# Seven quarter products for the gates and ups of a SwiGLU, and its second product in four parts

## The chip, the core and the metric

The kernel runs on one core of a Trainium2 chip. The metric is the device time of one execution, in microseconds (us). Before the change it is 2462.51 us, the median of 3 runs (2462.24 to 2464.69). The profile comes from one further execution, of 2461.3 us.

The core has a matrix engine, TensorE (PE in the profile, with its weight loads as PEld), and four others: VectorE (DVE), ScalarE (ACT), GpSimd (POOL) and SyncE (SP), whose queue issues the transfers from memory here. Each engine runs its own instructions in order and waits on semaphores for the others. A matmul multiplies a stationary 128x128 block (the weight load) with a moving block of 128 rows and up to 512 columns, and adds into a bank of PSUM of 128x512 floats.

## The reference

Two layers of a streaming encoder, 512 tokens, 1024 channels, in single precision. What bears on the change is the feed-forward block, which stands at the start and at the end of each layer, four times in all:

```
x = x + 0.5 * swiglu(rms_norm(x, norm_ffn1[l]), ffn1_wi[l], ffn1_wo[l])
...
def swiglu(x, w_in, w_out):
    gate, up = jnp.split(x @ w_in, 2, axis=-1)
    return (jax.nn.silu(gate) * up) @ w_out
```

Here w_in is 1024 x 5632 (2816 gates and 2816 ups) and w_out is 2816 x 1024. Between the two feed-forward blocks of a layer stand a mixer (a recurrent part, attention in chunks and a pooling) and a cross attention; the change leaves them as they are.

## The kernel before

Everything is kept channels by tokens: x is eight tiles of 128 channels x 512 tokens. Products in full precision are made of three matmuls: each operand is split into a high part (`hi`, a copy on ScalarE into the type F32R) and the rest (`lo`, a subtraction on VectorE), and `mm3` (L155) adds hi·hi, hi·lo and lo·hi into one bank. `split` (L140) makes such a pair, and every split of a 128x512 tile is one instruction on ACT and one on DVE. All instructions of the helpers show under the helper's line: L69 (`tt`, two tensors on DVE), L72 (`stt`, a tensor times a scalar, then a tensor), L75 (`act`), L78 (`mm`).

`ffn` (L261) works as follows. `norm` (L249) splits x times the gains into eight pairs (`hhi`, `hlo`); the tokens' factor 1/rms is left out here, is worked out while the first products run (`rstd`, L236), and is multiplied in afterwards, as the tile `r`. Then come 22 values of f, one for each 128 hidden channels. For each, `proj` makes the gates (`pg`) and then the ups (`pu`): `weights` (L144) loads 128 x 1024 weights in one transfer of 512 KB into one of two `raw` tiles, splits them in two halves of 512 columns into `whi` and `wlo` (three buffers each), and eight times three matmuls with 512 moving columns follow. So one f is 48 matmuls of 128x512. DVE multiplies both banks with `r`, ACT takes the silu, DVE multiplies gate and up, and the result is split into `fhi` and `flo`, kept for all 22 f. After the last f, the second product goes over the eight output tiles m: 22 times three matmuls into `po`, then `update` (L215), which adds half of the bank to x[m], stores it for ffn1, and starts the sum of squares for the next norm (a square on ACT, an addition on POOL).

The instructions are not issued in the order in which the code writes them. The framework's scheduler lists them when the program is built: on each engine what is ready comes first, and of several ready ones that which the code wrote first; a tile's buffer is given out again when its last reader is done. Each engine then keeps to that list. So the splits of the next weights are listed between the epilogue's instructions of the f before. The tiles `raw` (2 buffers), `whi` and `wlo` (3 each), the scratch tiles `t` (8) and the PSUM banks (8, by the tags in `ROT`, L92) set how far ahead the list can go.

Of the kernel before, what the change touches and what calls it, by code (L numbers as in the profile page):

```python
# [9 lines left out]
F32R = mybir.dt.float32r  # L10
AF = mybir.ActivationFunctionType
# [3 lines left out]
P = 128  # L15
T = 512
D = 1024
DEPTH = 2
KD = 8
FF = 2816  # L20
KF = FF // P
# [9 lines left out]
REL_MAX = 256  # L31
LEAD, DENSE_RATE, ATT_RATE = 15, (1.0, 0.61, 0.98), 0.65
TURN_RATE = (0.5, 0.9)

PAR = {}
_n = 0
# [17 lines left out]
def trunk(tc, I, out, depth=DEPTH):  # L54
    nc = tc.nc
    ctx = ExitStack()
    with ctx:
        const = ctx.enter_context(tc.tile_pool(name="const", bufs=1))
        wp = ctx.enter_context(tc.tile_pool(name="wp", bufs=1))
# [6 lines left out]
        mult, add, sub = ALU.mult, ALU.add, ALU.subtract  # L66

        def tt(o, a, b, op, eng=None):
            (eng or nc.vector).tensor_tensor(out=o, in0=a, in1=b, op=op)  # L69

        def stt(o, a, s, b, op0, op1):
            nc.vector.scalar_tensor_tensor(out=o, in0=a, scalar=s, in1=b, op0=op0, op1=op1)  # L72

        def act(o, i, f, **k):
            nc.scalar.activation(out=o, in_=i, func=f, **k)  # L75

        def mm(o, w, x, start=True, stop=True):
            nc.tensor.matmul(o, lhsT=w, rhs=x, start=start, stop=stop)  # L78

        def t2(name, shape=None, dt=F32):  # L80
            return tp.tile(shape or [P, T], dt, tag="t", name=name, bufs=8)
# [4 lines left out]
        def xslot(name):  # L86
            return hp.tile([P, T], F32, tag="x", name=name, bufs=8)

        def bank(tag, name):
            return psp.tile([P, T], F32, tag=tag, name=name, bufs=1 if tag in ("po", "ch") else 2)  # L90

        ROT = ("acc", "iv", "sm", "po", "acc", "iv", "sm", "ch")  # L92

        def b2(name):
            return bp.tile([P, T], F32, tag="b", name=name, bufs=6)
# [14 lines left out]
        x = [xslot("x") for _ in range(KD)]  # L110
        ahead = []

        def load_raw(ap, n, step=1024):
            raw = wp.tile([P, 1024], F32, tag="raw", name="raw", bufs=2)
            for c in range(0, n, step):
                nc.sync.dma_start(out=raw[:, c:min(c + step, n)], in_=ap[:, c:min(c + step, n)])
            return raw
# [9 lines left out]
        def pc(l, n, j=0):  # L127
            o, w = PAR[n]
            return par[:, l, o + j:o + j + 1]
# [10 lines left out]
        def split(o_hi, o_lo, src):  # L140
            act(o_hi, src, AF.Copy)
            tt(o_lo, src, o_hi.bitcast(F32), sub)
# [12 lines left out]
        def mm3(p, w, v, first, last):  # L155
            (wh, wl), (vh, vl) = w, v
            mm(p, wh, vh, first, False)
            mm(p, wh, vl, False, False)
            mm(p, wl, vh, False, last)

        def proj_steps(p, ap, nk, acts, first=True, last=True):
            done = 0
            for k0 in range(0, nk, 8):
                n = min(8, nk - k0)
                w = weights(ap[:, k0:k0 + n].rearrange("p k m -> p (k m)"), n * P)
                for k in range(n):
                    s = slice(k % 4 * P, k % 4 * P + P)
                    hi, lo = w[k // 4]
                    mm3(p, (hi[:, s], lo[:, s]), acts[k0 + k], first and done == 0, last and done == nk - 1)
                    done += 1  # L170
                    if k % 2:
                        yield
# [19 lines left out]
        def proj(*a, **k):  # L192
            for _ in proj_steps(*a, **k):
                pass
# [8 lines left out]
        def square_in(k):  # L203
            if k == 0:
                a = tp.tile([P, T], F32, tag="ssa", name="ssa", bufs=1)
                act(a, x[k], AF.Square)
                ssq["a"] = a
            else:
                q = t2("sq")
                act(q, x[k], AF.Square)  # L210
                tt(ssq["a"], ssq["a"], q, add, nc.gpsimd)

        x_dram = dram.tile([KD, P, T], F32, name="xs")

        def update(k, p, scale=None, spill=False, fetch=None):  # L215

            if fetch is not None:
                x[k] = fetch
                nc.sync.dma_start(out=x[k], in_=x_dram[k])
            if scale is None:  # L220
                tt(x[k], x[k], p, add)
            else:
                stt(x[k], p, scale, x[k], mult, add)
            if spill:
                nc.sync.dma_start(out=x_dram[k], in_=x[k])
            square_in(k)
# [9 lines left out]
        def rstd(bcast=True, tag="sm"):  # L236

            rt = const.tile([P, 4], F32, tag="rtok", name="rtok", bufs=1)
            tok_rstd(ssq["a"], T, rt, 1.0, eps, tag)
            r = None  # L240
            if bcast:
                p = bank(tag, "psn")
                for i in range(4):
                    mm(p[:, i * P:(i + 1) * P], rt[:, i:i + 1].to_broadcast([P, P]), ident)
                r = tp.tile([P, T], F32, tag="rstd", name="rstd", bufs=1)
                act(r, p, AF.Copy)
            return r, rt

        def norm(l, gain):  # L249
            h = []  # L250
            for k in range(KD):
                g = pc(l, gain, k)
                hi = hslot("hhi")
                act(hi, x[k], AF.Copy, scale=g)
                lo = hslot("hlo")
                stt(lo, x[k], g, hi.bitcast(F32), mult, sub)
                h.append((hi, lo))
            return h


        def ffn(l, which):  # L261
            h = norm(l, f"norm_{which}")
            wi, wo = I[f"{which}_wi"][l], I[f"{which}_wo"][l]
            hid = []
            with tc.tile_pool(name="hid", bufs=1) as hidp:
                for f in range(KF):
                    pg = bank(ROT[2 * f % 8], "pg")
                    proj(pg, wi[2 * f], KD, h)
                    pu = bank(ROT[(2 * f + 1) % 8], "pu")
                    proj(pu, wi[2 * f + 1], KD, h)  # L270
                    if f == 0:
                        if which == "ffn1" and l == 0:
                            for k in range(KD):
                                square_in(k)
                        r, _ = rstd(tag="po")
                    z = t2("z")
                    tt(z, pg, r, mult)
                    act(z, z, AF.Silu)
                    u = t2("u")
                    tt(u, pu, r, mult)  # L280
                    tt(u, u, z, mult)
                    hi = hidp.tile([P, T], F32R, name=f"fhi{f}")
                    lo = hidp.tile([P, T], F32R, name=f"flo{f}")
                    split(hi, lo, u)
                    hid.append((hi, lo))
                for m in range(KD):
                    p = bank(ROT[(m + 4) % 8], "po")
                    proj(p, wo[m], KF, hid)
                    update(m, p, 0.5, spill=which == "ffn1")

        vf_dram = dram.tile([3, P, T], F32, name="vf")

# [505 lines left out]
        def cross(l):  # L798
            with tc.tile_pool(name=f"cx{l}", bufs=1) as cp:
# [151 lines left out]
                while live:  # L951
                    blocked = False
                    if "d" in live:
                        got = next(live["d"], live)
                        blocked = got is True
                        if got is live:
                            del live["d"]
                    credit += TURN_RATE[len(k) == 8]
                    while "a" in live and (credit >= 1 or blocked or "d" not in live):
# [17 lines left out]
        for l in range(depth):  # L977
            ffn(l, "ffn1")
            mixer(l)
            cross(l)  # L980
            ffn(l, "ffn2")
# [94 lines left out]
```

## Time and profile before

| What | Value |
|---|---|
| Median of the runs | 2462.51 us |
| The profiled execution | 2461.3 us, of which the span from the first instruction to the last is 2459.5 |
| PE busy | 2422.8 us, 14058 matmuls |
| DVE busy | 1296.4 us, 2361 instructions |
| ACT busy | 999.4 us, 1800 instructions |
| POOL busy | 190.1 us, 246 instructions |
| Read from memory, written | 215.89 MB, 7.08 MB |
| Granted TensorE clock | 0.998 of full speed |

The feed-forward blocks are easy to find in the trace, by the tiles `pg`, `pu` and `po`: 7 to 375 us, 868 to 1229, 1229 to 1590 and 2095 to 2456 us. A row of the trace's timeline gives an instruction's start, its duration, its engine and line, what it writes and reads, and in brackets how long the engine had been idle before it and what it had waited for. Matmuls overlap, so one takes 0.39 us from start to end while the next starts after 0.227 us; for a rate, starts are compared, or the chain of waits is read, whose rows give a start, a length and a count.

### The profile page before, as it was taken

The page shows a single profiled execution, that of the slowest core. Times are in us where ns is not written, and L with a number is a line of the kernel's source. Part 1 is how long each engine was busy: PE and PEld are TensorE (multiplying, and loading weights), DVE is VectorE, ACT ScalarE, POOL GpSimd, SP SyncE. Part 2 cuts the span into 40 slices and gives each one's busy share as a digit, 9 for nine tenths or more (in the row PEclk, how much of TensorE's full clock was granted, in tenths as well). Part 3 has the DMA queues.
Part 4 walks back from the last instruction along what each step waited for, and adds up shares of the span by engine and source line. Part 5 has one row for each costly group of instructions (what it writes and reads, how often), then busy time and mean ns, then how long its engine had stood idle before and what let it go on. Part 6 is the DMA issues. An engine that isn't in the chain of part 4 may idle for free.

```text
span 2459.5 us, 35629 instructions
## 1 busy us (share of the span) xinstructions
PE 2422.8 (99%) x14058; PEld 1997.1 (81%) x14058; DVE 1296.4 (53%) x2361; ACT 999.4 (41%) x1800; POOL 190.1 (8%) x246
## 2 busy tenths in 40 slices
PE   8999999999999999999999999999999999999999
PEld 6888887787689888888888888867876898888887
DVE  5444335767675644443444443367676755444432
ACT  4333334444465543333333333343444655433322
POOL 1000002101110100000000000021011101000000
PEclk9999999999999999999999999999999999999999
DMA  4233333210242223333333233322103422232333
GB/s 136 95 95 103 107 112 108 70 44 21 79 146 90 71 95 96 102 95 94 95 98 99 95 94 119 120 73 69 46 21 92 140 82 78 93 99 94 97 109 95
DMA packets 72503, 225.27 MB, mean 92 GB/s; under 512 B 8176, under 2 KB 13200, under 8 KB 72336
## 3 DMA queue, kind: packets, MB, share of 16 engines
q1 hardware_dynamic: 72336, 223.00, 28.8%
q8 instruction: 110, 1.80, 0.3%
q14 instruction: 57, 0.47, 0.1%
HBM read 215.89 MB, written 7.08 MB: 91 GB/s over the span
## 4 chain that ended last, share of the span: by engine, by line
PE 94%; DVE 3%; issue 1%; DMA 1%; ACT 1%; POOL 0%; POOLq 0%; ACTq 0%; DVEq 0%; SPq 0%
PE pu L78 20%; PE po L78 19%; PE pg L78 19%; PE pxq L78 5%; PE pin L78 4%; PE pout L78 3%; PE pxw L78 3%; PE pqk L78 3%; PE pxv L78 2%; PE pbvf L78 1%; PE pf L78 1%; PE ptt L78 1%; DVE wlo L69 1%; PE pr L78 1%; PE pxs L78 1%; PE pxo L78 1%
## 5 line engine op out<-in xcount | busy, mean ns | idle before, releaser
L75 ACT ACTIVATE whi<-raw 128x512 fp32r<-128x512 f32 (+1 forms) x806 | 492.5, 613 | 966.2 <-PE po L78 288.1
L69 DVE TENSOR_TENSOR wlo<-raw,whi 128x512 fp32r<-128x512 f32 (+1 forms) x806 | 551.4, 687 | 553.4 <-ACT whi L75 544.3
L78 PE MATMUL pg<-hhi,whi 128*128 128x512 f32 x704 | 275.6, 392 | 6.7 <-ACT whi L75 6.7
L78 PE MATMUL pg<-hlo,whi 128*128 128x512 f32 x704 | 275.6, 391 | 2.2 <-DVE hlo L72 2.2
L78 PE MATMUL pg<-hhi,wlo 128*128 128x512 f32 x704 | 274.7, 390 | 0.0
L78 PE MATMUL pu<-hhi,wlo 128*128 128x512 f32 x704 | 274.0, 389 | 0.7 <-DVE wlo L69 0.7
L78 PE MATMUL pu<-hlo,whi 128*128 128x512 f32 x704 | 273.9, 389 | 0.0
L78 PE MATMUL pu<-hhi,whi 128*128 128x512 f32 x704 | 273.9, 389 | 0.0
L78 PE MATMUL po<-fhi,whi 128*128 128x512 f32 x704 | 273.9, 389 | 0.0
L78 PE MATMUL po<-flo,whi 128*128 128x512 f32 x704 | 273.9, 389 | 0.0
L78 PE MATMUL po<-fhi,wlo 128*128 128x512 f32 x704 | 273.9, 389 | 0.0
L69 POOL TENSOR_TENSOR ssa<-ssa,sq 128x512 f32<-128x512 f32 x63 | 86.6, 1374 | 1221.3 <-ACT sq L75 1220.8
L78 PEld LDWEIGHTS pg<-hhi,whi 128*128 128x128 f32 x704 | 132.8, 189 | 34.2 <-ACT whi L75 6.7
L78 PEld LDWEIGHTS pg<-hlo,whi 128*128 128x128 f32 x704 | 132.6, 188 | 31.5 <-DVE hlo L72 4.7
L78 PEld LDWEIGHTS pu<-hhi,wlo 128*128 128x128 f32 x704 | 132.2, 188 | 28.6 <-DVE wlo L69 1.2
L78 PEld LDWEIGHTS pg<-hhi,wlo 128*128 128x128 f32 x704 | 132.6, 188 | 27.6 <-DVE wlo L69 0.3
L78 PEld LDWEIGHTS po<-fhi,wlo 128*128 128x128 f32 x704 | 132.2, 188 | 27.5
L78 PEld LDWEIGHTS po<-flo,whi 128*128 128x128 f32 x704 | 132.2, 188 | 27.5
L78 PEld LDWEIGHTS pu<-hlo,whi 128*128 128x128 f32 x704 | 132.2, 188 | 27.4
L78 PEld LDWEIGHTS pu<-hhi,whi 128*128 128x128 f32 x704 | 132.1, 188 | 27.4
L78 PEld LDWEIGHTS po<-fhi,whi 128*128 128x128 f32 x704 | 132.2, 188 | 27.3
L69 DVE TENSOR_TENSOR z<-pg,rstd 128x512 f32<-128x512 f32 x88 | 60.9, 692 | 133.9 <-PE pg L78 124.3
(305 smaller groups left out, 3971.9 us busy)
## 6 DMA issues: line engine op xcount, KB each, us to landing
raw<-in_ffn_wi_dram SPq DMA_DIRECT2D x175, 512.0 KB, 3.5
raw<-in_ffn_wo_dram SPq DMA_DIRECT2D x64, 512.0 KB, 3.5
raw<-in_w_in_dram SPq DMA_DIRECT2D x30, 512.0 KB, 3.5
raw<-in_ffn_wo_dram SPq DMA_DIRECT2D x32, 384.0 KB, 3.2
raw<-in_x_wk_dram SPq DMA_DIRECT2D x16, 512.0 KB, 3.5
raw<-in_x_wv_dram SPq DMA_DIRECT2D x16, 512.0 KB, 3.6
raw<-in_x_wq_dram SPq DMA_DIRECT2D x16, 512.0 KB, 3.6
raw<-in_w_qk_dram SPq DMA_DIRECT2D x12, 512.0 KB, 3.6
```

Source lines behind the costliest of these rows:

```text
L69: (eng or nc.vector).tensor_tensor(out=o, in0=a, in1=b, op=op)
L75: nc.scalar.activation(out=o, in_=i, func=f, **k)
L78: nc.tensor.matmul(o, lhsT=w, rhs=x, start=start, stop=stop)
```

## The change

For 20 of the 22 f (the first two stay as they were, `PLAIN`), gates and ups are made by a form of Strassen's algorithm. The weights of one f are a 2x2 matrix of blocks: gates and ups (rows) by channels 0 to 511 and 512 to 1023 (columns). The normed x is a 2x2 matrix too: the two halves of the channels by the two halves of the tokens. Eight quarter products become seven, at the cost of sums: `token_sums` forms four combinations of x (once for each block, eight split pairs `thi`, `tlo`), and `seven` forms four combinations of the weights for each f, splits seven blocks (`shi`, `slo`, seven buffers), runs seven products of 4 x 3 matmuls with 256 moving columns (`Q`), and combines the results on DVE while it reads the banks (`z`, `v`, `u`).

The second product is cut into four parts by f (`PARTS`: 0 to 4, 5 to 10, 11 to 16, 17 to 21). The part of some f runs beside the gates and ups of the next group: `seven` is a generator with seven stops, and from the fifth stop of a group (`WO_LEAD`) each stop lets `second` go one step, two f of one output tile. The last part stands alone at the end. Each part adds to x[m] by two DVE instructions, and the tokens' factor `r` comes in there (`seven` and `plain` leave it out of the ups). The hidden tiles are now a ring of 11 buffers instead of 22 tiles.

The diff, with lines cut that the text above says:

```diff
+PARTS, PLAIN, WO_RATE, WO_LEAD = (0, 5, 11, 17, 22), 2, 1.0, 4
...
+        Q = T // 2
+
         def ffn(l, which):
             h = norm(l, f"norm_{which}")
             wi, wo = I[f"{which}_wi"][l], I[f"{which}_wo"][l]
-            hid = []
             with tc.tile_pool(name="hid", bufs=1) as hidp:
-                for f in range(KF):
+                hid = []
+                r = None
+
+                def out(z, u):
+
+                    hi = hidp.tile([P, T], F32R, tag="fhi", name="fhi", bufs=11)
+                    lo = hidp.tile([P, T], F32R, tag="flo", name="flo", bufs=11)
+                    split(hi, lo, u)
+                    hid.append((hi, lo))
+
+                def plain(f):
+                    nonlocal r
                     pg = bank(ROT[2 * f % 8], "pg")
                     proj(pg, wi[2 * f], KD, h)
...
-                    tt(u, pu, r, mult)
+                    tt(u, pu, z, mult)
+                    out(z, u)
...
+                def token_sums():
+                    for k in range(4):
+                        ga, gb = pc(l, f"norm_{which}", k), pc(l, f"norm_{which}", k + 4)
+                        xa, xb = x[k], x[k + 4]
+                        b1 = t2("b1")
+                        act(b1, xa, AF.Copy, scale=ga)
+                        s1, s2 = t2("s12"), t2("s34")
+                        stt(s1[:, :Q], xa[:, Q:], ga, b1[:, :Q], mult, sub)
+                        stt(s1[:, Q:], xb[:, Q:], gb, s1[:, :Q], mult, sub)
+                        stt(s2[:, :Q], xb[:, Q:], gb, b1[:, Q:], mult, sub)
+                        stt(s2[:, Q:], xb[:, :Q], gb, s1[:, Q:], mult, sub)
+                        for s in (s1, s2):
+                            hi = hidp.tile([P, T], F32R, tag="thi", name="thi", bufs=8)
+                            lo = hidp.tile([P, T], F32R, tag="tlo", name="tlo", bufs=8)
+                            split(hi, lo, s)
+                            sums.append((hi, lo))
...
+                def seven(f):
+
+                    ra, rb = [load_raw(wi[2 * f + i].rearrange("p k m -> p (k m)"), 1024) for i in range(2)]
+                    a11, a12, a21, a22 = ra[:, :T], ra[:, T:], rb[:, :T], rb[:, T:]
+
+                    def parts(src):
+                        hi = hidp.tile([P, T], F32R, tag="shi", name="shi", bufs=7)
+                        lo = hidp.tile([P, T], F32R, tag="slo", name="slo", bufs=7)
+                        split(hi, lo, src)
+                        return hi, lo
+
+                    def sums_of(a, b, op):
+                        s = t2("ws")
+                        tt(s, a, b, op)
+                        return s
+
+                    def product(n, p, c, w):
+
+                        for k, v in enumerate(quarter(n)):
+                            s = slice(k * P, k * P + P)
+                            mm3(p[:, c * Q:c * Q + Q], (w[0][:, s], w[1][:, s]), v, not c and k == 0, (c or n == 1) and k == 3)
...
+                    w1 = parts(a11)
+                    w2 = parts(a12)
+                    s1 = sums_of(a21, a22, add)
+                    s2 = sums_of(s1, a11, sub)
+                    w6 = parts(s2)
+                    s4 = sums_of(a12, s2, sub)
+                    w3 = parts(s4)
+                    s3 = sums_of(a11, a21, sub)
+                    w7 = parts(s3)
+                    w5 = parts(s1)
+                    w4 = parts(a22)
+                    pa = bank("acc", "p1")
+                    product(1, pa, 0, w1)
+                    p1 = t2("p1")
+                    act(p1[:, :Q], pa[:, :Q], AF.Copy)
+                    yield
+                    pb = bank("iv", "p26")
+                    product(2, pb, 0, w2)
+                    yield
+                    product(6, pb, 1, w6)
+                    z = t2("z")
+                    tt(two(z), two(pb), twice(p1, 0), add)
+                    yield
+                    pb = bank("acc", "p37")
+                    product(3, pb, 0, w3)
+                    yield
+                    product(7, pb, 1, w7)
+                    v = t2("v")
+                    tt(two(v), two(pb), twice(z, 1), add)
+                    yield
+                    pb = bank("sm", "p54")
+                    product(5, pb, 0, w5)
+                    yield
+                    product(4, pb, 1, w4)
+                    tt(z[:, Q:], pb[:, :Q], v[:, :Q], add)
+                    tt(z, z, r, mult)
+                    act(z, z, AF.Silu)
+                    u = t2("u")
+
+                    tt(two(u)[:, ::-1], two(pb), twice(v, 1), add)
                     tt(u, u, z, mult)
...
+                    out(z, u)
+                    yield
+
+                def second(f0, f1, last, tags):
+
+                    for m in range(KD):
+                        p = bank(tags[m % len(tags)], "po")
+                        for g0 in range(f0, f1, 4):
+                            n = min(4, f1 - g0)
+                            raw = b2("wr")
+                            nc.sync.dma_start(out=raw[:, :n * P], in_=wo[m][:, g0:g0 + n].rearrange("p k m -> p (k m)"))
...
+                            split(hi[:, :n * P], lo[:, :n * P], raw[:, :n * P])
+                            for k in range(n):
+                                s = slice(k * P, k * P + P)
+                                mm3(p, (hi[:, s], lo[:, s]), hid[g0 + k], g0 + k == f0, g0 + k == f1 - 1)
+                                if k % 2:
+                                    yield
+                        t = t2("po")
+                        stt(t, p, 0.5, r, mult, mult)
+                        tt(x[m], x[m], t, add)
...
+                        yield
+
+                wos, credit = iter(()), 0
+                for f0, f1 in zip(PARTS, PARTS[1:]):
+                    for f in range(f0, f1):
+                        if f < PLAIN:
+                            plain(f)
+                            if f == 0:
+                                token_sums()
+                            continue
+                        for _ in seven(f):
+                            credit += WO_RATE
+                            while credit >= 1:
+                                credit -= 1
+                                next(wos, None)
+                    for _ in wos:
+                        pass
+                    wos, credit = second(f0, f1, f1 == KF, ("po", "ch") if f1 < KF else ROT[4:] + ROT[:4]), -WO_LEAD
+                for _ in wos:
+                    pass
```

More of the change, by code (lines that the diff above doesn't have):

```diff
@@ L279, in ffn @@
                     u = t2("u")
-                    tt(u, pu, r, mult)
-                    tt(u, u, z, mult)
[L282 to L289, printed above, removed]
+                    tt(u, pu, z, mult)
@@ new lines, in plain @@
+                    out(z, u)
+                sums = []
+                def token_sums():
[14 more added lines that the diff above has]
+                            sums.append((hi, lo))
@@ new lines, in quarter, with twice @@
+                def quarter(n):
+                    at = {1: (0, 0), 2: (4, 0), 3: (4, 1)}
+                    if n in at:
+                        k0, c = at[n]
+                        t = h[k0:k0 + 4]
+                    else:
+                        i, c = {5: (0, 0), 6: (0, 1), 7: (1, 0), 4: (1, 1)}[n]
+                        t = sums[i::2]
+                    return [(hi[:, c * Q:c * Q + Q], lo[:, c * Q:c * Q + Q]) for hi, lo in t]
+                def seven(f):
[14 more added lines that the diff above has]
+                            mm3(p[:, c * Q:c * Q + Q], (w[0][:, s], w[1][:, s]), v, not c and k == 0, (c or n == 1) and k == 3)
+                    def twice(t, c):
+                        return t[:, c * Q:c * Q + Q].unsqueeze(1).to_broadcast([P, 2, Q])
+                    two = lambda t: t.rearrange("p (c t) -> p c t", c=2)
+                    w1 = parts(a11)
[37 more added lines that the diff above has]
+                    tt(two(u)[:, ::-1], two(pb), twice(v, 1), add)
+                    tt(u, u, z, mult)
+                    out(z, u)
+                    yield
@@ new lines, in second @@
+                def second(f0, f1, last, tags):
[5 more added lines that the diff above has]
+                            nc.sync.dma_start(out=raw[:, :n * P], in_=wo[m][:, g0:g0 + n].rearrange("p k m -> p (k m)"))
+                            hi = wp.tile([P, 512], F32R, tag="whi", name="whi", bufs=3)
+                            lo = wp.tile([P, 512], F32R, tag="wlo", name="wlo", bufs=3)
+                            split(hi[:, :n * P], lo[:, :n * P], raw[:, :n * P])
[7 more added lines that the diff above has]
+                        tt(x[m], x[m], t, add)
+                        if last:
+                            if which == "ffn1":
+                                nc.sync.dma_start(out=x_dram[m], in_=x[m])
+                            square_in(m)
+                        yield
```

## The prediction, made before the changed kernel ran

> **What bounds the kernel now.** I read the page first: the busy shares, the slices and the shares of the chain that ended last.
>
> ```profile
> PE 2422.8 (99%) x14058; PEld 1997.1 (81%) x14058; DVE 1296.4 (53%) x2361; ACT 999.4 (41%) x1800; POOL 190.1 (8%) x246
> ...
> PE   8999999999999999999999999999999999999999
> PEld 6888887787689888888888888867876898888887
> DVE  5444335767675644443444443367676755444432
> ...
> PE 94%; DVE 3%; issue 1%; DMA 1%; ACT 1%; POOL 0%; POOLq 0%; ACTq 0%; DVEq 0%; SPq 0%
> ```
>
> PE is the chain. A busy PE need not stream at its rate, so the chain of waits in order of time comes next; its columns are start, length, what, count.
>
> ```profile
> 867.89 5.44 PE pg L78 x24
> 873.33 5.44 PE pu L78 x24
> 886.10 5.44 PE pu L78 x24
> ...
> 1109.14 119.68 PE po L78 x528
> ...
> 1942.42 5.51 PE pxq L78 x46
> ...
> 1973.91 14.87 PE pxq L78 x124
> ```
>
> A 512-column matmul takes 5.44 / 24 = 0.2267 us, and `po` has the same rate over 528 of them. A plain f (48 matmuls) is 10.88 us, a second product 119.68. A feed-forward block thus runs at PE's rate, with 1.9 us lost once, at `rstd` (886.10 less 878.77, less one 5.44). The last two rows price what the change adds: with 256 moving columns and a 128x128 weight load each, `pxq` runs at 14.87 / 124 = 0.1199 us.
>
> The table by stretches says how much of the other engines is free.
>
> ```profile
> core 0: us, PE busy (x) PEld busy (x) DVE busy (x) ACT busy (x) POOL busy (x), PEclk, DMA share, GB/s
> ...
> 1229.00:1470.00 241.00, 241.00 (x1073) 199.84 (x1072) 114.36 (x176) 86.70 (x138) 1.29 (x1) 1.00 0.31 97
> ```
>
> During gates and ups DVE is busy under half the time, and the clock is granted in full. Since the change loads DVE heavily, I looked at its timeline over one f (start, duration, instruction, idle before).
>
> ```profile
> 206.38 0.69 DVE L69 TENSOR_TENSOR z<-pg,rstd 128x512 f32<-128x512 f32 x1 [1.53 <-PE pg L78]
> 206.99 0.68 DVE L69 TENSOR_TENSOR wlo<-raw,whi 128x512 fp32r<-128x512 f32 x1
> 209.60 0.69 DVE L69 TENSOR_TENSOR wlo<-raw,whi 128x512 fp32r<-128x512 f32 x1 [1.93 <-ACT whi L75]
> 211.82 0.69 DVE L69 TENSOR_TENSOR u<-pu,rstd 128x512 f32<-128x512 f32 x1 [1.53 <-PE pu L78]
> 212.43 0.68 DVE L69 TENSOR_TENSOR wlo<-raw,whi 128x512 fp32r<-128x512 f32 x1
> 213.03 0.69 DVE L69 TENSOR_TENSOR u<-u,z 128x512 f32<-128x512 f32 x1
> 214.42 0.69 DVE L69 TENSOR_TENSOR flo<-u,fhi 128x512 fp32r<-128x512 f32 x1 [0.70 <-ACT fhi L75]
> 215.04 0.69 DVE L69 TENSOR_TENSOR wlo<-raw,whi 128x512 fp32r<-128x512 f32 x1
> ```
>
> Eight instructions per f. One lasts 0.69 us, but the next, where it doesn't depend on it, starts 0.605 us later (211.82, 212.43, 213.03). So 0.605 is the price in a dense row, 0.69 in a chain. The order also shows that the next weights' splits stand between the epilogue's instructions: the scheduler works ahead.
>
> **What PE saves.** A seven-product f has 7 x 12 = 84 matmuls of 256 columns: 84 x 0.1199 = 10.07 us against 10.88, a saving of 0.81. Over 20 f and four blocks: 80 x 0.81 = 64.6 us. The seventh product is worth less than an eighth because a half-wide matmul costs 53% of a whole one. The cheaper bound is exactly half, 0.1133 (1.36 us per f, 109 in all); the dearer would be serial weight loads, which the rate of `pxq` excludes. I take `pxq`: same types, same loads, same width.
>
> [...]
>
> The second product keeps its matmuls (4 parts, the same 528 of 512 columns), so it costs PE the same wherever it stands.
>
> **What DVE and ACT gain.** One seven-product f: 7 splits and 4 sums of weights, then `z`, `v`, half of `z`, `z` times `r`, `u`, `u` times `z`, `flo`: 17.5 instructions of 512 columns, 10.6 us at 0.605. Where no second product runs beside it, that is more than PE's 10.07. ACT has nine of these and a 256-column copy, by the rows below 9 x 0.63 + 0.42 = 6.1 us: hidden.
>
> ```profile
> 842.14 0.42 DVE L69 TENSOR_TENSOR wlo<-raw,whi 128x256 fp32r<-128x256 f32 x1
> ...
> 841.62 0.42 ACT L75 ACTIVATE whi<-raw 128x256 fp32r<-128x256 f32 x1 [1.26 <-DMA raw<-in_x_wo_dram]
> ...
> L75 ACT ACTIVATE fhi<-u 128x512 fp32r<-128x512 f32 x88 | 55.6, 632 | 124.6 <-DVE u L69 124.6
> ...
> L72 DVE SCALAR_TENSOR_TENSOR xk<-pxqt,par,xk 128x256 fp32r<-128x256 f32 x16 | 7.7, 482 | 3.5 <-ACT xk L75 3.5
> ```
>
> One step of the second product adds six matmuls, 1.36 us of PE; a whole m of six f is 4.08 us of PE over four steps and on DVE a split of 512, one of 256 (0.42 less the same overlap, 0.34), and two instructions of the update: 2.2 us. So a filled f (seven steps) is PE 10.07 + 7.1 = 17.2, DVE 10.6 + 3.8 = 14.4; with five-f parts 18.0 and 15.3. PE binds there. The steps: a part of five f has 8 x 3 = 24, one of six 8 x 4 = 32. Four stops of each group pass first, so unfilled are f = 2 to 4 (nothing to run yet), four stops of f = 5, f = 9 and 10, then six and four stops around f = 11 and 16, four at f = 17: some 7.6 f per block.
>
> **Where it stalls.** Both `raw` tiles now belong to one f. The second can be loaded again only when its last reader, the split of a22, is done.
>
> ```profile
> 20.93 3.46 DMA raw<-in_ffn_wi_dram
> ...
> SPq L116 <- DVE wlo L69: 1923.5, 386, 30.0
> ```
>
> The first row (chain of waits) is such a load on the path; the second says that SP's queue usually stands waiting for DVE to let go of a tile. So in an unfilled f there is a turn: load 3.5 us; then, before a22's split ends, nine weight instructions, `z`, `v` and two or three of the previous f's end, 13.5 x 0.605 = 8.2; and 0.7 for the chain s1, s2, ACT, `slo`, in which DVE finds less to do. That is 12.4 against PE's 10.07: PE loses 2.4 us per unfilled f once the slack is used. In a filled f the turn is some 3.5 us longer, 15.9, below PE's 17.2: slack grows again.
>
> At the start of a block comes the backlog of `token_sums`. By the 256-column row above (0.48 in a chain) one k is 4 x 0.48 + 2 x 0.605 = 3.1 us, four are 12.5. The rows there:
>
> ```profile
> 870.44 1.34 DVE L72 SCALAR_TENSOR_TENSOR hlo<-xs,par,hhi 128x512 fp32r<-128x512 f32 x1 [0.71 <-ACT hhi L75]
> ...
> 869.94 1.29 POOL L69 TENSOR_TENSOR ssa<-ssa,sq 128x512 f32<-128x512 f32 x1 [4.67 <-ACT sq L75]
> ```
>
> PE gives two plain f and `rstd`, 2 x 10.88 + 1.9 = 23.7 us; DVE has to do the last update and `hlo` (2), two times eight (9.7), the sums (12.5): 24.2. So DVE comes to f = 2 with nothing in hand beyond the first two splits. PE wants the split for product 6 after 2.88 us; three weight instructions, two of f = 1's end and ACT's copy make about 4.1: stall 1.2. The split of a22 is then done at 23.7 + 14 x 0.605 + 0.7 = 32.9, the load at 36.4, product 6's pair 4.2 later at 40.6 (3.0 for the chain, two instructions of f = 2's end ahead of it), where PE would be at 23.7 + 1.2 + 10.07 + 2.88 = 37.9: stall 2.7. Then 2.4 each at f = 4 and f = 5; from f = 6 on the fill restores slack. Sum 8.7 per block. At f = 9 to 11 and later I count none: three filled f save over 4 us, a tile's lead of one f, before two unfilled ones spend it.
>
> At the end of a block m follows m after 15 x 0.2267 = 3.4 us instead of 15, with 0.6 (split) + 0.2 + 1.2 (update) + 0.7 (`hlo`) of DVE, and POOL's 1.29 us addition beside it, during which `hlo` took 1.34. Close to balance: 1.5 us lost, bounds 0 and 4. The update's second instruction puts the last `hlo` at about 4 us behind the last matmul; the next stage's 21 matmuls of k = 0 to 6 (4.76 us) hide that. The hidden ring is no wait: f = 16 overwrites f = 5's buffer, whose readers end six stops earlier.
>
> Sum, against the profiled execution: 2461.3 - 64.6 + 4 x (8.7 + 1.5) = 2461.3 - 64.6 + 40.8 = 2437.5; the median stands 1.2 above it: **2438.7**.
>
> **The rivals.** (1) The scheduler hides the turn and the backlog, since lists put splits into every gap and PE can run other ready products; then only the end of a block costs: 2461.3 - 64.6 + 6 = 2402.7, so 2403.9 at the median. For it: before, PE never waits in these stages. Against: DVE has 10.6 us to do in 10.07.
>
> (2) Slower: the turn binds in the filled f too. SP's queue issues in order, and the second product's small loads (64 per block, where there were 24), each waiting for its own scratch tile, stand ahead of the `raw` load. If that puts 2 us on the turn, a filled turn is 15.9 + 2 = 17.9, with the ends' 0.7 of added chain 18.6 against 17.6 on average: 1.0 lost in each of some 13 f, and 2.4 in the unfilled 6 to 7: 29 per block, 2461.3 - 64.6 + 4 x 30.5 = 2519. It decides once filled turns pass 17.2; the change as a whole turns slower when a block loses over 16.2 us. For it: the long SP waits above. Against: 1.3 us of room.
>
> (3) Every DVE instruction costs its whole 0.69. Then an unfilled turn is 3.5 + 13.5 x 0.69 + 0.7 = 13.5 and a filled one 18.3: 3.4 x 6.5 + 0.7 x 13.5 = 32 per block, 2530. The starts at 0.605 speak against it. [...]
>
> (4) The matmuls don't get cheaper: 256 columns break even at 10.88 / 84 = 0.1295 us. If two readings of one bank or the mixing of widths costs that, 2461.3 + 41 = 2502. Every `pxq` row speaks against it.
>
> **How the numbers follow.** The forecast, with 4 to 14 us lost at the start and end of each block (2414 to 2454), 0.47; rival 1 0.27; rival 2 0.17; rival 3 0.04; rival 4 0.05. The range 2402 to 2500 takes in rival 1, the forecast and the milder half of rival 2. Measurement tells 0.2%, about 4.9 us, from no change. Faster: rival 1, 0.42 of the forecast, 0.02 of the others: 0.71. Within: 0.07. Slower: 0.22.
>
> **What would show it.** Right: matmuls of `p26`, `p37`, `p54` 0.120 us apart; PE idle a few us before product 6 of f = 3, 4 and 5 of each block, released by `slo` or DVE, with DVE dense and a `raw` load ending just before `ws`; no idle PE in filled f; DVE busy about 2000 us. Wrong: PE waiting in filled f (rival 2), starts on DVE 0.69 apart (3), matmuls at 0.13 (4), or no idle PE at all (1).

## The result and the profile after

The changed kernel takes 2476.06 us, the median of 4 runs (2474.78 to 2477.6), beside 2462.38 us for the kernel before, the median of 4 (2457.64 to 2464.69). The ratio is 1.0058, with an interval of 1.0041 to 1.0076: slower by 14 us, where the prediction had 24 faster. The helpers' lines are one higher than before (L70 `tt`, L73 `stt`, L76 `act`, L79 `mm`). First the page of the kernel after.

```profile
span 2475.8 us, 43241 instructions
...
PE 2397.7 (97%) x16938; PEld 2080.2 (84%) x16938; DVE 1929.0 (78%) x3537; ACT 1161.6 (47%) x2232; POOL 188.6 (8%) x246
...
PE   7999999999999989999989999999999999899999
...
PE 83%; DVE 10%; issue 2%; ACT 2%; DMA 2%; POOL 0%; POOLq 0%; ACTq 0%; DVEq 0%; SPq 0%
```

DVE has gone from 3% to 10% of the chain that ended last, and PE from 94% to 83%. The slices of PE dip at the start of the four blocks (7, 8, 8, 8). Laid out by blocks, from the first `pg` to the last `po`:

| Block | before | after |
|---|---|---|
| 1 | 368.1 | 369.3 |
| 2 | 360.9 | 362.7 |
| 3 | 360.9 | 364.9 |
| 4 | 360.9 | 361.6 |

The blocks are 7.5 us longer together instead of 64.8 shorter (80 x 0.81), so 72.3 us are lost inside them, and 8.8 more outside: 7.0 in the stretches from a block's last `po` to the next block's first `pg`, and 1.8 at the end of the kernel. Where the 72.3 lie, by the gaps between starts of successive matmuls beyond 0.1199 us (256 columns) and 0.2267 (512): f = 2 33.5 over the four blocks, f = 3 to 6 15.1, f = 12 5.4, the other seven-product f 9.7 (0.1 to 0.3 each), the last part of the second product 5.8, 2.6 at the start of block 3, which follows block 2 directly, and 0.2 in the plain f of block 1.

**The largest loss, f = 2.** The table by stretches of the kernel after, at the start of the second block (columns: length, busy time of PE, PEld, DVE, ACT and POOL with counts, granted clock, DMA share, GB/s):

```profile
880.00:892.00 12.00, 12.00 (x62) 10.17 (x61) 4.79 (x8) 6.81 (x10) 0.00 (x0) 1.00 0.24 82
892.00:898.00 6.00, 6.00 (x30) 5.03 (x29) 5.83 (x12) 4.90 (x10) 0.00 (x0) 1.00 0.44 129
898.00:904.00 6.00, 2.97 (x23) 2.54 (x22) 6.00 (x15) 3.92 (x7) 0.00 (x0) 1.00 0.00 0
904.00:910.00 6.00, 3.22 (x7) 2.14 (x8) 5.96 (x12) 2.72 (x6) 0.00 (x0) 0.57 0.17 50
```

Up to 892 us DVE is busy 40% of the time (4.79 of 12 us); from then on it is full, and only then PE runs dry. The work was there to be done earlier. What held it is in ACT's timeline of the same kernel:

```profile
891.44 0.63 ACT L76 ACTIVATE z<-z 128x512 f32<-128x512 f32 x1
...
892.60 0.71 ACT L76 ACTIVATE b<-xs,par 128x512 f32<-128x512 f32 x1
...
893.73 0.71 ACT L76 ACTIVATE b<-xs,par 128x512 f32<-128x512 f32 x1
```

`b<-xs,par` is the first step of `token_sums` for one k. It needs nothing but x, which was complete at 875.2, yet the first one starts at 892.60, 18.8 us into the block (which starts at 873.81), just behind the silu of f = 0. And the chain of waits:

```profile
891.44 0.64 ACT z L76
...
892.17 0.09 DVE u L70
...
893.41 0.89 DVE s L73 x2
...
905.18 0.68 DVE tlo L70
...
906.06 0.68 DVE u L70
...
906.78 3.45 PE po L79 x7
...
911.89 6.72 PE p L79 x56
```

So from 893 to 906 the path runs through DVE (`s`, `tlo`), and f = 1's `u` stands behind the sums. By the code's tags it frees the bank of PSUM that the next `po` use. PE's timeline has PE idle for 5.81 us before them, until that `u`:

```profile
906.78 0.80 PE L79 MATMUL po<-fhi,whi 128*128 128x512 f32 x1 [5.81 <-DVE u L70]
```

Then the clock: seven `po` of 512 columns take 3.45 us there, 0.49 each, where 56 `p` of 256 columns after 911.89 take 0.1200 each as predicted. The granted clock is 0.50 for 6.83 us from 904.86 on (0.57 over 904 to 910 above), and for as long in the same place of all four blocks; of the 8.4 us that f = 2 loses, some 2.4 are that (the starts in this stretch against 0.2267 and 0.1199).

**The end of a block.** First the timeline of POOL, whose addition closes each output tile, then that of DVE for two tiles, both of the kernel after:

```profile
1221.34 1.29 POOL L70 TENSOR_TENSOR ssa<-ssa,sq 128x512 f32<-128x512 f32 x1 [2.76 <-ACT sq L76]
1225.39 1.30 POOL L70 TENSOR_TENSOR ssa<-ssa,sq 128x512 f32<-128x512 f32 x1 [2.76 <-ACT sq L76]
1229.45 1.30 POOL L70 TENSOR_TENSOR ssa<-ssa,sq 128x512 f32<-128x512 f32 x1 [2.76 <-ACT sq L76]
```

```profile
1219.05 0.68 DVE L73 SCALAR_TENSOR_TENSOR po<-po,rstd 128x512 f32<-128x512 f32 x1
...
1221.43 1.36 DVE L70 TENSOR_TENSOR wlo<-wr,whi 128x128 fp32r<-128x128 f32 x1 [0.30 <-ACT whi L76]
1222.71 0.68 DVE L73 SCALAR_TENSOR_TENSOR po<-po,rstd 128x512 f32<-128x512 f32 x1
1223.31 0.68 DVE L70 TENSOR_TENSOR wlo<-wr,whi 128x512 fp32r<-128x512 f32 x1
1223.91 0.68 DVE L70 TENSOR_TENSOR xs<-xs,po 128x512 f32<-128x512 f32 x1
1224.51 0.74 DVE L73 SCALAR_TENSOR_TENSOR hlo<-xs,par,hhi 128x512 fp32r<-128x512 f32 x1
1225.90 1.34 DVE L73 SCALAR_TENSOR_TENSOR hlo<-xs,par,hhi 128x512 fp32r<-128x512 f32 x1 [0.65 <-ACT hhi L76]
1227.16 0.68 DVE L73 SCALAR_TENSOR_TENSOR po<-po,rstd 128x512 f32<-128x512 f32 x1
```

A tile comes every 4.06 us (1221.34, 1225.39, 1229.45) where PE needs 3.4. Two of the DVE instructions above start while POOL's addition runs, and both end shortly behind it: the split of 128 columns 0.16 us (1222.79, where POOL ends at 1222.63), `hlo` 0.55 us (1227.24, 1226.69). They take 1.36 and 1.34 us, where the same instructions take 0.28 (at 1219.65) and 0.74 (at 1224.51) without it. DVE falls behind tile by tile, and the next block pays at its start. The chain of waits there:

```profile
1242.71 1.34 DVE hlo L73
...
1244.09 0.73 PE pg L79 x2
```

The last `hlo` ends at 1244.05, 7.5 us behind the last matmul of the block (which starts at 1236.27; 0.23 more is an estimate of its end by the rate of 0.2267); the prediction had about 4, hidden by 4.76 us of other matmuls.

### The profile page after: what moved, and what is told of

Read it like the earlier page. It is cut to its first block, busy times and chain, and to the rows that moved or that the text cites. A ratio compares the mean times of both kernels' runs of the same rounds, so it can differ in the third digit from the quotient of the medians.

```text
span 2475.8 us, 43241 instructions
## 1 busy us (share of the span) xinstructions
PE 2397.7 (97%) x16938; PEld 2080.2 (84%) x16938; DVE 1929.0 (78%) x3537; ACT 1161.6 (47%) x2232; POOL 188.6 (8%) x246
## 4 chain that ended last, share of the span: by engine, by line
PE 83%; DVE 10%; issue 2%; ACT 2%; DMA 2%; POOL 0%; POOLq 0%; ACTq 0%; DVEq 0%; SPq 0%
PE p L79 29%; PE po L79 18%; PE pxq L79 6%; PE pin L79 4%; PE pxw L79 3%; PE pout L79 3%; PE pqk L79 3%; DVE wlo L70 2%; PE pbvf L79 1%; PE pu L79 1%; PE pf L79 1%; PE ptt L79 1%; DVE ws L70 1%; DVE s L73 1%; PE pg L79 1%
## 5 line engine op out<-in xcount | busy, mean ns | idle before, releaser
L79 PE MATMUL p<-thi,shi 128*128 128x256 f32 x1280 | 365.1, 286 | 5.1 <-ACT shi L76 5.0
L79 PE MATMUL p<-thi,slo 128*128 128x256 f32 x1280 | 360.0, 284 | 2.3 <-DVE slo L70 2.3
L79 PE MATMUL p<-tlo,shi 128*128 128x256 f32 x1280 | 361.4, 283 | 0.0
L70 DVE TENSOR_TENSOR wlo<-raw,whi 128x512 fp32r<-128x512 f32 (+3 forms) x294 | 209.7, 722 | 122.1 <-ACT whi L76 110.6
L79 PE MATMUL po<-fhi,whi 128*128 128x512 f32 x704 | 278.7, 400 | 25.1 <-DVE u L70 22.8
L79 PE MATMUL po<-fhi,wlo 128*128 128x512 f32 x704 | 278.3, 396 | 2.9 <-DVE wlo L70 2.5
L79 PE MATMUL po<-flo,whi 128*128 128x512 f32 x704 | 280.1, 398 | 0.0
L76 ACT ACTIVATE whi<-raw 128x512 fp32r<-128x512 f32 (+3 forms) x294 | 175.0, 602 | 215.8 <-PE pin L79 50.9
L79 PE MATMUL p<-hlo,shi 128*128 128x256 f32 x960 | 271.9, 283 | 0.0
L79 PE MATMUL p<-hhi,shi 128*128 128x256 f32 x960 | 271.9, 283 | 0.0
L79 PE MATMUL p<-hhi,slo 128*128 128x256 f32 x960 | 271.6, 283 | 0.0
L79 PEld LDWEIGHTS p<-thi,shi 128*128 128x128 f32 x1280 | 244.5, 191 | 30.7 <-ACT shi L76 23.5
L79 PEld LDWEIGHTS p<-thi,slo 128*128 128x128 f32 x1280 | 243.4, 191 | 10.3 <-DVE slo L70 6.6
L79 PEld LDWEIGHTS p<-tlo,shi 128*128 128x128 f32 x1280 | 244.9, 191 | 4.4
L76 ACT ACTIVATE shi<-ws 128x512 fp32r<-128x512 f32 x320 | 191.9, 627 | 120.3 <-DVE ws L70 118.5
L76 ACT ACTIVATE whi<-wr 128x512 fp32r<-128x512 f32 (+2 forms) x256 | 125.1, 492 | 247.0 <-PE po L79 160.2
L70 POOL TENSOR_TENSOR ssa<-ssa,sq 128x512 f32<-128x512 f32 x63 | 86.3, 1370 | 1775.9 <-ACT sq L76 1435.3
L70 DVE TENSOR_TENSOR slo<-ws,shi 128x512 fp32r<-128x512 f32 x320 | 210.6, 686 | 4.5 <-ACT shi L76 4.0
L70 DVE TENSOR_TENSOR wlo<-wr,whi 128x512 fp32r<-128x512 f32 (+2 forms) x256 | 143.7, 563 | 62.0 <-ACT whi L76 61.6
L76 ACT ACTIVATE shi<-raw 128x512 fp32r<-128x512 f32 x240 | 141.8, 622 | 101.2 <-DMA raw<-in_ffn_wi_dram 101.0
L79 PEld LDWEIGHTS p<-hhi,shi 128*128 128x128 f32 x960 | 183.6, 191 | 5.5 <-ACT shi L76 1.0
L79 PEld LDWEIGHTS p<-hlo,shi 128*128 128x128 f32 x960 | 183.8, 191 | 4.2
```

## The experiments

Theory A: the sums of f = 2 come late because the scratch ring `t` (8 buffers) is given out in the order in which the code asks, and `b1`, `s12` and `s34` ask behind `z` and `u` of f = 0, which wait for 1/rms. Theory B, the prediction's own: DVE simply has more to do at the start than PE gives it time for. A second question is what sets the period of an unfilled f (12.4 us), a third what the end costs.

**e1: own tiles for the sums.** They take buffers of `shi` and `slo`, which nothing uses yet.

```diff
-                        b1 = t2("b1")
+                        b1 = hidp.tile([P, T], F32, tag="slo", name="b1", bufs=7)
...
-                        s1, s2 = t2("s12"), t2("s34")
+                        s1, s2 = [hidp.tile([P, T], F32, tag="shi", name=n, bufs=7) for n in ("s12", "s34")]
```

> The changed kernel, only that token_sums takes its scratch tiles from the rings of shi and slo, which stand empty then, instead of from the ring t. Theory A: PE loses 8.4 us at f = 2 of each block because the ring t is handed out in the order in which the code asks: the first sum stands behind z and u of f = 0, and these wait for rstd, so DVE lies idle for some 15 us and has all sums to do at once. Then the first sum starts about 3 us after the block instead of 19, but ahead of the splits for f = 1, since the code writes it first: the loss goes from 8.4 to 3 to 6 us, 2455 to 2467 us in all. Theory B: the 12.5 us of sums are simply too much work for DVE before f = 2, whatever the order: 2473 to 2479 us.

Measured: 2464.12 us beside 2461.39, ratio 1.0014 (1.0004 to 1.0023). The loss of f = 2 fell from between 8.0 and 8.8 us per block to 0.3, so the ring was what held the sums. But now they are listed ahead of f = 1's weight splits, and the two plain f lose 18.4, 2.8, 4.7 and 4.5 us in the four blocks, where they lost 7.6, 0.2, 2.8 and 0.2. Freed from one place, the work stood in another place's way.

**e1b: the same, and the sums asked for after f = 1.**

```diff
-                            if f == 0:
+                            if f == 1:
                                 token_sums()
```

> As e1_own_tiles, and the sums are written behind f = 1 instead of f = 0, so that the splits for f = 1 go first and the sums fill DVE's gaps. Theory A: the loss at f = 2 falls from 8.4 to about 1.5 us per block, the stretches of half clock in the blocks go, 2476 - 28 = 2448 us. Theory B: 2473 to 2479 us, with the half clock still there.

Measured: 2447.11 us beside 2461.39, ratio 0.9947 (0.993 to 0.9964). ACT's timeline and the stretch of f = 2 in this kernel, whose second block begins at 868.97:

```profile
866.82 0.71 ACT L76 ACTIVATE b<-xs,par 128x512 f32<-128x512 f32 x1
...
873.72 0.71 ACT L76 ACTIVATE b<-xs,par 128x512 f32<-128x512 f32 x1
```

```profile
894.00:900.00 6.00, 6.00 (x42) 5.28 (x41) 5.89 (x10) 3.87 (x8) 0.00 (x0) 1.00 0.25 65
900.00:906.00 6.00, 6.00 (x52) 6.00 (x51) 3.95 (x7) 1.31 (x3) 0.00 (x0) 1.00 0.46 162
```

These are the first and the last of the four `b`: they start 2.2 us ahead of the block and 4.8 us into it, where in the change they start 18.8 and 25.5 us into it (899.32). PE has no gap, the clock stays at 1.00, and f = 2 loses 0.4 (2.8 in the first block). The plain f lose 1.0 us more per block (1.7 in the first, 0.6 in the third). DVE does the same work, so theory B falls: it was never too much, it was late. The gain over the change is 29 us.

**e3: one instruction for the last update.** The factor `r` goes into the hidden tiles of the last part again, and x[m] gets half of the bank in one instruction.

```diff
                     tt(u, u, z, mult)
+                    if f >= PARTS[-2]:
+                        tt(u, u, r, mult)
                     out(z, u)
...
-                        t = t2("po")
-                        stt(t, p, 0.5, r, mult, mult)
-                        tt(x[m], x[m], t, add)
+                        if last:
+                            stt(x[m], p, 0.5, x[m], mult, add)
+                        else:
+                            t = t2("po")
+                            stt(t, p, 0.5, r, mult, mult)
+                            tt(x[m], x[m], t, add)
```

> The changed kernel, only that the last part's hidden tiles are multiplied by r (one DVE instruction for each of five f), and so the last update is one DVE instruction per output tile instead of two. Theory: at the end of a block DVE sets the pace, 4.06 us per output tile against PE's 3.4; 0.6 less makes it 3.46, and the 4.4 us lost per block there and at the start of the next stage become about 1: 2476 - 14 = 2462 us. Rival: the pace is set by POOL's additions and by ACT's order, so output tiles still come every 4.0 us or more: 2473 to 2479 us.

Measured: 2462.82 us beside 2461.39, ratio 1.0007 (0.9997 to 1.0016), 13 us faster than the change. DVE's timeline of this kernel:

```profile
1213.27 0.68 DVE L73 SCALAR_TENSOR_TENSOR xs<-po,xs 128x512 f32<-128x512 f32 x1
...
1216.72 0.68 DVE L73 SCALAR_TENSOR_TENSOR xs<-po,xs 128x512 f32<-128x512 f32 x1
...
1220.17 0.68 DVE L73 SCALAR_TENSOR_TENSOR xs<-po,xs 128x512 f32<-128x512 f32 x1
```

A tile every 3.45 us, close to PE's own 3.40; the last part loses 0.1 us per block instead of 0.5 to 1.8, and the 2.6 at the start of block 3 are gone. One DVE instruction less per output tile, 32 in all (and 20 more beside the last gates and ups, where there is room), was worth 13 us. What a single profile cannot settle is how much of the rest lies outside the blocks: the stretches between blocks are 495 and 502 us here, 498 and 507 in the change, 493 and 505 in the kernel before.

**e5: the parts alone.** All 22 f stay plain, and no sums are made; the second product still comes in four parts.

```diff
-PARTS, PLAIN, WO_RATE, WO_LEAD = (0, 5, 11, 17, 22), 2, 1.0, 4
+PARTS, PLAIN, WO_RATE, WO_LEAD = (0, 5, 11, 17, 22), 22, 1.0, 4
...
-                            if f == 0:
-                                token_sums()
```

> The four-part second product alone: all 22 f are made the old way (eight quarter products, no sums of tokens), and each part runs behind its group. If the end of the block is what the parts cost, 4.4 us per block: 2462.4 + 18 = 2480 us. If the parts cost nothing by themselves and all losses come from the seven products: 2462 us.

Measured: 2478.53 us beside 2461.39, ratio 1.0073 (1.0058 to 1.0088). The parts alone cost 17 us, with DVE busy only 1402.1 us, so it isn't DVE's total that costs. Most of it lies at the blocks' ends, as e3 suggests: in e5's trace 5.5 us are lost in the last parts, 2.8 at the start of block 3 and 1.8 at the end of the kernel. The seven products on top of them bring 2.5 us of their 64.8.

**e7: e1b and e3 together.**

> The sums' own scratch tiles behind f = 1 (as e1b) and the single update in the last part (as e3) together. The two losses lie at opposite ends of a block, so the gains add: 2476 - 29 - 13 = 2434 us, faster than both kernels. If one gain only moves a wait that the other had hidden, 2440 us or more.

Measured: 2437.55 us beside 2461.28 (2431.94 to 2438.12), ratio 0.99 (0.9886 to 0.9915). This beats both kernels, by 24 us and by 38. The two remedies alone came to 29 and 13, so together they fall short of their sum by about 4, which is no more than the uncertainty (the interval of the ratio is 7 us wide). What is left in the blocks: 17.9 us in the first (7.3 of them were lost before the change), 9.3, 8.9 and 10.2 in the others, of which f = 3 to 6 make 3.1 and f = 12 1.4 to 2.5.

The next three start from e7 and ask about the period of an unfilled f. The row of one in e7 (f = 10 of the second block), in the table by stretches, whose counts take in matmuls that reach over its ends:

```profile
1004.75:1017.15 12.40, 12.40 (x95) 11.68 (x94) 11.01 (x18) 5.51 (x10) 0.00 (x0) 1.00 0.27 88
```

12.40 us as predicted, but PE isn't idle: besides the 84 matmuls of the f it runs about nine `po`, which the scheduler listed there.

**e8: the ups' weights in two transfers, into another ring.** If the `raw` tile sets the turn, this should shorten it.

```diff
-                    ra, rb = [load_raw(wi[2 * f + i].rearrange("p k m -> p (k m)"), 1024) for i in range(2)]
-                    a11, a12, a21, a22 = ra[:, :T], ra[:, T:], rb[:, :T], rb[:, T:]
+                    ra = load_raw(wi[2 * f].rearrange("p k m -> p (k m)"), 1024)
+                    wu = wi[2 * f + 1].rearrange("p k m -> p (k m)")
+                    a21, a22 = b2("a21"), b2("a22")
+                    nc.sync.dma_start(out=a21, in_=wu[:, :T])
+                    nc.sync.dma_start(out=a22, in_=wu[:, T:])
+                    a11, a12 = ra[:, :T], ra[:, T:]
```

> As e7_both, and the ups' weights of each f are loaded in two halves of 256 KB into two tiles of the ring b (six buffers) instead of into the second raw tile, so the load for the next f no longer waits for the last split of this one. Theory of the prediction (the raw tiles' turn of 12.4 us sets the unfilled f): f = 3 to 5 come every 11 us instead of 12.3, and 4 to 12 us are gained in all: 2422 to 2430. Rival: the turn is set by the ring t, because the first weight sum of an f asks for its tile behind the u of the f before: f = 3 to 5 still come every 12.3 us, 2431 to 2437.

Measured: 2453.21 us beside 2461.28, ratio 0.997 (0.9959 to 0.9982), 16 us worse than e7. f = 9 in this kernel:

```profile
996.80:1009.85 13.05, 10.59 (x86) 10.18 (x85) 12.24 (x22) 6.56 (x12) 0.00 (x0) 1.00 0.21 71
```

84 matmuls in 13.05 us, 2.5 of them idle: the turn got no shorter, and no `po` fills it any more. None of the 80 first weight sums waits for a load here. That the second product's weights now stand behind the ups' in one ring is the likely reason; it wasn't tried by itself.

**e9: the four sums of the weights in the other ring, `raw` as it was.**

```diff
-                        s = t2("ws")
+                        s = b2("ws")
```

> As e7_both, and the weight sums take their tiles from the ring b instead of t, so they need not wait for the u of the f before; the raw tiles stay two. If the ring t sets the turn of the unfilled f: f = 3 to 5 under 12 us, 2422 to 2430. If the raw load sets it: 12.3 us as before, 2431 to 2437; the second product's loads now stand behind the sums in ring b, which may cost some of PE's filling.

Measured: 2439.45 us beside 2461.28, ratio 0.9913 (0.9898 to 0.9927), the same as e7 within its uncertainty. f = 9 and 10 of the first block:

```profile
148.45:158.53 10.08, 10.08 (x86) 10.08 (x85) 9.24 (x16) 3.84 (x7) 0.00 (x0) 1.00 0.18 54
158.53:168.60 10.07, 10.07 (x86) 10.07 (x85) 9.33 (x16) 4.26 (x9) 0.00 (x0) 1.00 0.43 145
```

With the loads untouched, these two f take 10.08 and 10.07 us with PE full. DVE's timelines show the difference, at the start of f = 10 of the second block; first e7, then e9:

```profile
1005.09 0.68 DVE L70 TENSOR_TENSOR u<-p,v 128x512 f32<-128x512 f32 x1
...
1006.28 0.69 DVE L70 TENSOR_TENSOR ws<-raw 128x512 f32<-128x512 f32 x1
```

```profile
1004.08 0.69 DVE L70 TENSOR_TENSOR ws<-raw 128x512 f32<-128x512 f32 x1
...
1005.46 0.69 DVE L70 TENSOR_TENSOR v<-p,z 128x512 f32<-128x512 f32 x1
...
1008.81 0.68 DVE L70 TENSOR_TENSOR u<-p,v 128x512 f32<-128x512 f32 x1
```

In e7 the first sum of the next weights stands behind `u` of the f before, because both take their tile from ring `t` in the order of the code; in e9 it runs 4.7 us ahead of that `u`. So in the change and in e7 the ring sets the turn: of the 80 first sums (one for each seven-product f) none in the change and one in e7 waits for a `raw` load. In e9 22 of them do, among them those of f = 10 and f = 11 of the first block, in DVE's timeline:

```profile
155.18 0.69 DVE L70 TENSOR_TENSOR ws<-raw 128x512 f32<-128x512 f32 x1 [0.74 <-DMA raw<-in_ffn_wi_dram]
...
167.25 0.69 DVE L70 TENSOR_TENSOR ws<-raw 128x512 f32<-128x512 f32 x1 [0.71 <-DMA raw<-in_ffn_wi_dram]
```

They are 12.07 us apart (12.0 to 12.3 in the other blocks). The load's turn is thus real and nearly as long as the ring's, which hid it. PE runs at 10.07 here only by a lead that it spends: the first sum starts 11.9 us ahead of its f at f = 9, 3.2 at f = 10 and 1.3 at f = 11. Where there is no lead, at f = 4 of the second to fourth block, the first sum waits 0.6 to 0.9 us for its load. So the time is no better: the `po` that filled the 12.4 us now stand elsewhere, and f = 4 and 5 lose 1.9 to 4.1 each instead of 0.9 and 1.3. e8 takes only the turn of the ups' load away and e9 only the ring's; no run takes away both.

**e6: no pace.** The stops of `seven` no longer call `second`; each part is asked for only behind the whole group of f that it ran beside.

```diff
-PARTS, PLAIN, WO_RATE, WO_LEAD = (0, 5, 11, 17, 22), 2, 1.0, 4
+PARTS, PLAIN, WO_RATE, WO_LEAD = (0, 5, 11, 17, 22), 2, 0.0, 4
```

> As e7_both with WO_RATE 0: the second product's parts are no longer let in step by step, each is written whole behind the next group. If the scheduler's own filling of PE's gaps is enough, 2434 us as e7_both. If the pace written by hand matters, the products of a group run unfilled, 12.3 us per f against 10.07 + little filling, and some 1.2 us for each of 14 f per block are lost: 2434 + 60 = about 2490 us.

Measured: 2562.03 us beside 2461.28, ratio 1.0408 (1.0393 to 1.0424), 124 us worse than e7, far beyond what was expected. f = 7 of the first block, and f = 11 of the second:

```profile
103.70:115.90 12.20, 10.73 (x86) 10.27 (x86) 11.01 (x19) 5.51 (x10) 0.00 (x0) 1.00 0.31 104
...
1034.20:1068.90 34.70, 34.70 (x195) 30.20 (x194) 27.23 (x48) 12.13 (x24) 0.00 (x0) 1.00 0.36 107
```

Left alone, the scheduler runs f = 7 to 10 without fill, at 12.2 to 13.8 us each, and then the part in one piece (108 `po` besides the 84 matmuls of f = 11). Here the turn is paid in full; the pace written by hand is what covers it. The mean granted clock is 0.98 here and 0.997 in e7; as an estimate from these means that is up to 44 of the 124 us (0.02 of 2561 less 0.003 of 2436); the last section shows one such place.

## Why the prediction was wrong

Its price list held. A `p` takes 0.1200 us (6.72 / 56 against 0.1199); the saving is 0.81 per f (e9's f in 10.07 us); instructions in a dense row of DVE start 0.60 us apart, which leaves nothing of rival 3; rival 4 falls with the 0.120; filled f lose 0.1 to 0.5 us, so rival 2, the queue of SP, falls too; DVE is busy 1929.0 us where about 2000 was said; f = 9 to 11 lose 0.1 to 0.3, as "I count none" had it. Its sum failed by 40 us in its terms (the four blocks of the profiled execution together):

| Term | predicted | measured |
|---|---|---|
| f = 2, behind the sums | 4.8 | 33.5 |
| f = 3 to 6 | 30 | 15.1 |
| End of the blocks and what follows | 6 | 17.2 |
| f = 12 | 0 | 5.4 |
| Other f | 0 | 9.7 |

The step that failed is "At the start of a block comes the backlog of `token_sums`". It compared DVE's work up to f = 2 (24.2 us) with PE's time (23.7), and took it that DVE starts on that work when the block starts. DVE's sums began 19.6 us into the block (893.41) and ended at 905.86, 32 us into it; the work was sized about right (12.45 us from the first to the last, with two other instructions among them, where 12.5 was said) and placed wrongly. The description of the kernel names the rings (`t` with 8 buffers among them) as what sets how far ahead a list can go; the prediction didn't ask from which ring the sums' tiles come and who asks before them. e1 shows that it is the ring, and e1b, which changes the order too, what the late start cost: 29 us. Of the 33.5 some 10 (2.3 to 2.8 in each block) are the halved clock behind the gap, for which the prediction had no term.

The second is the end of a block: "Close to balance: 1.5 us lost, bounds 0 and 4", and the last `hlo` hidden. It listed the right instructions, `hlo` at 0.7, and named POOL's addition, beside which `hlo` takes 1.34, but left that out of its sum: 0.6 + 0.2 + 1.2 + 0.7 is 2.7 us a tile, the instruction beside POOL adds 0.6 (`hlo`) to 1.1 (the small split), and ahead of it DVE waits 0.3 to 0.65 for ACT (the brackets of the rows), which comes to the measured period of about 4.06. The 17.2 us are 4.3 per block, just beyond its bound of 4; e3 takes 13 of them away. How the stretches between the blocks share in it stays open, as said there.

The third error lay on the other side, for f = 3 to 6. The turn of an unfilled f is 12.4 us, as worked out, but that the size fits is in part luck: in the change ring `t` sets it, not the `raw` load, whose own turn of 12.07 us shows only when the ring is out of the way (e9). And PE fills most of the turn with `po`, a mild form of rival 1. On the other hand f = 12 lost 1.35 per block where nothing was counted; e8 brings it to 0.3, and e9 to 0.1 or 0.2 in three blocks, so either edit takes it away, and which wait it was stays open.

The saving that was expected is therefore there: 64.8 us on PE. Against it stand 81 us of losses, 51 of them at two places in every block: an order of buffers, and one instruction too many. With both mended (e7), 24 us are gained, and some 41 of the 64.8 are still lost.

## What to carry to other kernels

When a change adds work that is meant to be done ahead, ask what it must be given before it can start: a tile from a shared ring is handed out in the order of the code, and one early request that waits for a late result holds all behind it. Count an engine's work from when it can start, not from when the stage does; an engine that is half idle just before it becomes the bound (busy 4.79 us of 12 here) is the sign in the profile. And a second instruction in a loop near balance can cost its whole length in every turn (4.06 us a tile here, 3.45 without it in e3), and again where the next stage waits for the last one (2.6 us at the start of block 3). Where an edit removes a wait and the time stays, look in its trace for the wait that took its place: of two turns of nearly the same length one can hide the other (12.4 and 12.07 us in e7 and e9).

## What the runs showed of the hardware

One is the granted clock behind short gaps of PE. In the change 6.83 us at 0.50 come with a gap of 5.81 us without a matmul (904.86 to 911.69, the first 1.9 of them still in the gap). In e6 the gaps are much shorter. PE's timeline of e6 in two successive f with the same gaps, and the table by stretches of the second:

```profile
985.15 0.39 PE L79 MATMUL p<-thi,shi 128*128 128x256 f32 x1 [0.91 <-ACT shi L76]
986.22 0.39 PE L79 MATMUL p<-thi,slo 128*128 128x256 f32 x1 [0.56 <-DVE slo L70]
997.33 0.39 PE L79 MATMUL p<-thi,shi 128*128 128x256 f32 x1 [0.91 <-ACT shi L76]
998.40 0.39 PE L79 MATMUL p<-thi,slo 128*128 128x256 f32 x1 [0.56 <-DVE slo L70]
```

```profile
997.00:999.00 2.00, 1.11 (x7) 0.90 (x8) 2.00 (x5) 1.71 (x4) 0.00 (x0) 1.00 0.00 0
999.00:1001.00 2.00, 2.00 (x13) 2.00 (x12) 1.90 (x4) 0.82 (x2) 0.00 (x0) 0.59 0.00 0
1001.00:1003.00 2.00, 2.00 (x12) 2.00 (x12) 1.74 (x3) 0.85 (x2) 0.00 (x0) 0.55 0.80 262
```

Behind gaps of 0.91 and 0.56 us (the brackets) the granted clock was 1.00 in every stretch from 985 to 997 us, and behind the same gaps in the next f 0.59 and 0.55 over 999 to 1003. That f took 13.56 us and the one before 12.18, so the lower clock behind 1.5 us of gaps cost 1.4 more. What decides between the two, no run here shows.

The other is DVE beside POOL's addition of about 1.3 us, at the end of every block. At the ends of the blocks of the kernel after, the 11 splits of 128 columns that start while an addition runs (0.09 to 0.20 us into it) end 0.15 or 0.16 us behind it, and the 15 `hlo` of 512 columns (0.50 to 0.52 us into it) 0.54 to 0.56 behind it; so an instruction of 0.28 us alone took up to 1.36. In the kernel before, an `hlo` that starts 0.20 us into the addition of 1185.78 takes 1.64 us and again ends 0.54 behind it, while `xs<-xs,pxw`, which has one input in PSUM, starts 0.46 us into an addition (2073.72) and takes 0.68 us, as it does elsewhere (0.67 to 0.69). `wlo<-wr,whi` and `hlo<-xs,par,hhi` both read two tiles in SBUF; whether that makes the difference, no run here shows.
